# A row gradient through one DMA queue: turns of three loads and three stores become turns of two and two

## The chip, the cores and the metric

The kernel runs on one core of a Trainium2 chip. The metric is device time in microseconds of one execution, the median of several runs. A core has several engines that run on their own and wait for one another by semaphores. Four matter here: VectorE (DVE), which does the arithmetic; GpSimd (POOL), which does some tiny pieces; SyncE (SP), which only issues transfers; and the 16 DMA engines, which move data between the device memory and the core's on-chip memory.

## The reference

The input is an array `x` of 8192 x 8192 float32 values. The output is its gradient along each row:

```python
def reference(x: np.ndarray) -> np.ndarray:
    return np.gradient(x, axis=1)
```

Inside a row, output `j` is `(x[j+1] - x[j-1]) / 2`. At the two ends of a row it is the plain difference of the two outermost values. Each value is read once and written once: 268.44 MB in and 268.44 MB out.

## The kernel before

The 8192 rows are cut into `nsets` = 32 groups of 256 rows. A group is a tile of 128 partitions with two whole rows in each (16384 values, 64 KB per partition), so one load or one store of a group moves 8.39 MB. In what follows, L7 and S7 are the load and the store of group 7, and a turn is a place where the queue passes from loads to stores or back. (Names such as L70 with a higher number are lines of the code, as the profile writes them.)

There are `NB` = 3 slots in on-chip memory, and group `i` uses slot `i % 3`. A slot is 64 values longer than a group (`SH`): the load puts the group at an offset of 64, and the result is written at offset 0 of the same slot, so the shift lets the result run behind the reading in place.

For each group the work is:

- POOL subtracts at the row ends and keeps the four differences per partition in `ends` (line 70). It waits for the load.
- DVE computes half the difference of the shifted rows for the whole group in one instruction (line 76). It waits for POOL's subtraction.
- The `ends` values are copied over the two end places of each row (line 87), by POOL for groups whose number leaves 1 or 3 after division by 5, and by DVE for the others.
- SP issues the store (line 89), after that copy.

All loads (line 60) and stores are issued by SP, in program order, and go through one queue. The DMA engines work this queue off in order, each engine for its own part of every transfer. When SP waits for something, everything behind that instruction on SP waits too. The dependences are written out by hand: `chain` names for each instruction the earlier ones it needs. A load of group `i` from 3 on needs the store of group `i - 3`, which had the same slot.

Lines 64, 65 and 91 to 93 set the order of the queue. The first three loads go out at the start; after the store of every third group the next three loads are issued. The queue thus holds L0 L1 L2 S0 S1 S2 L3 L4 L5 S3 S4 S5 and so on; at the end, 32 groups not being a multiple of three, come L30 L31 S30 S31.

Of the kernel before, what the change touches and what calls it, by code (L numbers as in the profile page):

```python
# [1 line left out]

# [4 lines left out]


@with_exitstack
def kernel(  # L10
    ctx: ExitStack,
    tc: tile.TileContext,
    x: bass.AP,
    out: bass.AP,
):

    nc = tc.nc
    P = nc.NUM_PARTITIONS
    n, m = x.shape
    R = 2
    NB = 3  # L30
    SH = 64  # L31
    W = R * m
    nsets = n // (P * R)
    f32 = x.dtype

    x_sets = x.rearrange("(s p t) m -> s p (t m)", p=P, t=R)
    out_sets = out.rearrange("(s p t) m -> s p (t m)", p=P, t=R)

    pool = ctx.enter_context(tc.tile_pool(name="pool", bufs=1))
    slots = [pool.tile([P, SH + W], f32, name=f"slot{k}", tag=f"slot{k}") for k in range(NB)]  # L40
    ends = pool.tile([P, nsets, R, 2], f32, name="ends", tag="ends")
    loads, stores = [], [None] * nsets
    in_front = {}

    def chain(i, ins, *needed):

        group, engine = f"slot{i % NB}", ins.ins.engine
        keep = [o.ins for o in needed]  # L50
        if in_front.get(engine, (None,))[0] == group:
            keep.append(in_front[engine][1])
        tc.declare_no_dep(ins.ins, group=group, keep=keep, reason="implied by the needed step")
        tc.add_to_no_dep_group(group, ins.ins)
        in_front[engine] = group, ins.ins
        return ins

    def load(i):
        b = slots[i % NB]
        ins = nc.sync.dma_start(out=b[:, SH : SH + W], in_=x_sets[i])  # L60
        loads.append(chain(i, ins, *([stores[i - NB]] if i >= NB else [])))

    with tc.manual_schedule():
        for i in range(NB):
            load(i)
        for i in range(nsets):
            b = slots[i % NB]
            xin = b[:, SH : SH + W].rearrange("p (t m) -> p t m", m=m)

            ins = nc.gpsimd.tensor_sub(  # L70
                out=ends[:, i, :, :],
                in0=xin[:, :, 1 : m : m - 2],
                in1=xin[:, :, 0 : m - 1 : m - 2],
            )
            at = [chain(i, ins, loads[i])]
            ins = nc.vector._custom_dve(  # L76
                dve_ops.TENSOR_TENSOR_REDUCE_SUB_MAX,
                out=b[:, 1 : W - 1],
                in0=b[:, SH + 2 : SH + W],
                in1=b[:, SH : SH + W - 2],  # L80
                s0=0.0,
                s1=0.5,
            )
            halved = chain(i, ins, *at)
            res = b[:, 0:W].rearrange("p (t m) -> p t m", m=m)
            placer = nc.gpsimd if i % 5 in (1, 3) and i < nsets - 2 else nc.vector
            ins = placer.tensor_copy(out=res[:, :, 0 : m : m - 1], in_=ends[:, i, :, :])  # L87
            placed = chain(i, ins, halved)
            ins = nc.sync.dma_start(out=out_sets[i], in_=b[:, 0:W])
            stores[i] = chain(i, ins, placed)  # L90
            if i % NB == NB - 1:
                for k in range(i + 1, min(i + 1 + NB, nsets)):
                    load(k)


# [1 line left out]
_INS = ['x']  # L97
_OUTS = [((8192, 8192), 'float32')]


# [23 lines left out]
```

## Time and profile before

| what | value |
| --- | --- |
| median of 3 runs | 1247.86 us (1247.71 to 1247.9) |
| profiled execution: its span, the only time that is recorded for it | 1245.7 us |
| DMA queue's packets, share of 16 engines' span | 99.8% |
| mean transfer rate | 431 GB/s |
| DVE busy | 554.6 us, 45% |
| one DVE instruction of line 76 | 17.22 us, 32 of them |
| POOL busy | 8.8 us, 1% |
| SP's queue waiting for a load's slot to be stored | 373.1 us in 29 waits |
| SP's queue waiting for a result, copied by DVE / by POOL | 525.6 us in 20 waits / 300.1 us in 12 |

A view in order of time has the start in microseconds from the beginning of the span, the duration, the engine, the line, the operation and the tiles; in brackets stands how long the engine was idle before and what ended it. "SPq" is SP issuing a transfer. "x3" or "x2" is a row in which two or three like instructions are merged, with the time from the first to the end of the last. A view by windows has, for each stretch of time, its length, the busy time of DVE and POOL with the number of instructions, the TensorE clock, the share of the DMA engines and the rate. A packet is 64 KB, one engine's eighth of its part of a transfer, and counts whole in the window where it starts, so a short window can show shares over 1 and rates far over the mean. The trace also keeps the start and duration of each single packet; where a text says "packet records", these are meant.

### The profile page before, as it was taken

Reading aid. Unit: us, or ns where it says so; the run is one execution under the profiler, and the core shown is the slowest. Engines: PE = TensorE matmul, PEld = TensorE weight load, DVE = VectorE, ACT = ScalarE, POOL = GpSimd, SP = SyncE. Lnnn points to the kernel's source line nnn. Section 1 sums busy time; section 2 is a strip of 40 time slices with the busy share of each in tenths; the row PEclk is TensorE's granted clock in tenths of the full one; section 3 lists DMA queues with packets and bytes.
Section 4 is the critical chain, followed back from the end, with each engine's and each line's share of the span. In section 5 each row is a group of like instructions: output and inputs, shape, how many; then the busy total and the mean of one; then the engine's idle time right before and its main releaser. Section 6 shows DMA issues by size and latency. Waiting matters only on the chain.

```text
span 1245.7 us, 237 instructions
## 1 busy us (share of the span) xinstructions
DVE 554.6 (45%) x52; POOL 8.8 (1%) x48
## 2 busy tenths in 40 slices
DVE  2850583069009702850582079009603840591083
POOL 0000000000000000000000000000000000000000
DMA  9999999999999999999999999999999999999999
GB/s 404 438 436 423 427 431 438 438 438 436 436 427 431 425 438 436 425 434 436 429 434 436 434 436 434 436 434 438 419 436 436 434 438 438 431 434 429 429 410 404
DMA packets 9217, 536.88 MB, mean 431 GB/s; under 512 B 1024, under 2 KB 1024, under 8 KB 1024
## 3 DMA queue, kind: packets, MB, share of 16 engines
q1 hardware_dynamic: 9216, 536.88, 99.8%
q14 instruction: 1, 0.01, 0.0%
HBM read 268.44 MB, written 268.44 MB: 431 GB/s over the span
## 4 chain that ended last, share of the span: by engine, by line
another core or an unknown queue 74%; DVE 18%; DMA 3%; issue 2%; POOL 1%; SPq 0%; POOLq 0%
DVE slot L76 18%; DMA slot<-in_x_dram 3%; POOL ends L70 0%; POOL slot L87 0%; SPq L60 0%; POOLq L119 0%; DVE slot L87 0%
## 5 line engine op out<-in xcount | busy, mean ns | idle before, releaser
L76 DVE CUSTOM_DVE_ANT_0 slot<-slot 128x16382 f32<-128x16382 f32 x32 | 551.2, 17224 | 668.7 <-POOL ends L70 668.7
L70 POOL TENSOR_TENSOR ends<-slot 128x4 f32<-128x4 f32 x32 | 6.3, 198 | 989.6 <-DMA slot<-in_x_dram 989.6
L87 POOL COPY slot<-ends 128x4 f32<-128x4 f32 x12 | 2.3, 190 | 207.9 <-DVE slot L76 207.9
L87 DVE COPY slot<-ends 128x4 f32<-128x4 f32 x20 | 3.4, 172 | 0.7
L108 POOL MEMSET const-bfloat16-1.0<- 128x1 bf16 x1 | 0.1, 101 | 0.0
L108 POOL MEMSET const-uint8-127<- 128x1 uint8 x1 | 0.1, 101 | 0.0
L108 POOL MEMSET const-float32-0.0<- 128x1 f32 x1 | 0.1, 98 | 0.2 <-issue 0.2
L108 POOL MEMSET const-float32-1.0<- 128x1 f32 x1 | 0.1, 98 | 0.0
## 6 DMA issues: line engine op xcount, KB each, us to landing
slot<-in_x_dram SPq DMA_DIRECT2D x32, 58.0
out_dram<-slot SPq DMA_DIRECT2D x32, 40.4
```

What stands on the lines that cost most here:

```text
L70: ins = nc.gpsimd.tensor_sub(out=ends[:, i, :, :], in0=xin[:, :, 1 : m : m - 2], in1=xin[:, :, 0 : m - 1 : m - 2],)
L76: ins = nc.vector._custom_dve(dve_ops.TENSOR_TENSOR_REDUCE_SUB_MAX, out=b[:, 1 : W - 1], in0=b[:, SH + 2 : SH + W], in1=b[:, SH : SH + W - 2],
L87: ins = placer.tensor_copy(out=res[:, :, 0 : m : m - 1], in_=ends[:, i, :, :])
L108: nc = _bacc.Bacc("TRN2", target_bir_lowering=False, num_devices=1)
```

## The change

The order of the queue is all that changes. `turns` is the list 2, 4, 6, ... 32. Two loads go out at the start, and after the store of every second group the next two loads are issued, so the queue holds L0 L1 S0 S1 L2 L3 S2 S3 and so on to L30 L31 S30 S31: 16 turns of two and two. There are still three slots, used in rotation, so a load of group `i` still needs the store of group `i - 3`. What the engines compute, the tiles, the size of a transfer and who copies the ends stay as they were.

```diff
@@ -31,6 +22,7 @@
     SH = 64
     W = R * m
     nsets = n // (P * R)
+    turns = list(range(2, nsets + 1, 2))
     f32 = x.dtype
 
@@ -61,7 +51,7 @@
         loads.append(chain(i, ins, *([stores[i - NB]] if i >= NB else [])))
 
     with tc.manual_schedule():
-        for i in range(NB):
+        for i in range(turns[0]):
             load(i)
         for i in range(nsets):
             b = slots[i % NB]
@@ -88,8 +78,8 @@
             placed = chain(i, ins, halved)
             ins = nc.sync.dma_start(out=out_sets[i], in_=b[:, 0:W])
             stores[i] = chain(i, ins, placed)
-            if i % NB == NB - 1:
-                for k in range(i + 1, min(i + 1 + NB, nsets)):
+            if i + 1 in turns[:-1]:
+                for k in range(i + 1, turns[turns.index(i + 1) + 1]):
                     load(k)
```

## The prediction

> **What bounds the kernel now.** I read the page first: busy shares, slices, queues. Then I read the instructions in order of time, for when each load lands and each store is issued, and last the busy time of narrow windows at two places where the queue turns from loads to stores. The page:
>
> ```profile
> span 1245.7 us, 237 instructions
> DVE 554.6 (45%) x52; POOL 8.8 (1%) x48
> DMA 9999999999999999999999999999999999999999
> q1 hardware_dynamic: 9216, 536.88, 99.8%
> L76 DVE CUSTOM_DVE_ANT_0 slot<-slot 128x16382 f32<-128x16382 f32 x32 | 551.2, 17224 | 668.7 <-POOL ends L70 668.7
> ```
>
> The one queue keeps the 16 DMA engines busy for 99.8% of the span, and VectorE works 45% of it. So the time is the time of 64 transfers of 8.39 MB, one after another, and the question is what the new order does to the gaps between them. The chain of waits gives 74% to an "unknown queue" and is no help here. In order of time, POOL's subtraction (L70) starts 0.07 us after its load has landed, so its starts are the landings:
>
> ```profile
> 489.13 0.20 POOL L70 TENSOR_TENSOR ends<-slot 128x4 f32<-128x4 f32 x1 [59.56 <-DMA slot<-in_x_dram]
> 508.46 0.20 POOL L70 TENSOR_TENSOR ends<-slot 128x4 f32<-128x4 f32 x1 [19.13 <-DMA slot<-in_x_dram]
> 528.31 0.20 POOL L70 TENSOR_TENSOR ends<-slot 128x4 f32<-128x4 f32 x1 [2.14 <-DMA slot<-in_x_dram]
> 605.63 0.20 POOL L70 TENSOR_TENSOR ends<-slot 128x4 f32<-128x4 f32 x1 [77.12 <-DMA slot<-in_x_dram]
> ```
>
> These are L12, L13, L14 and L15 (L and S are the load and store of a group). L13 follows L12 by 19.33 us. L14 follows by 19.85: 0.5 us more. L15 comes 77.32 us later, four transfers (S12, S13, S14, L15) of 19.33. Every triple looks so: only its last load, the one with a store behind it in the queue, is ever late. Over the nine triples from L5 to L29 the third interval is over 19.34 by 0.11, 0.17, 0.71, 0.51, 0.45, 0.11, 0.50, -0.01 and 0.02: 2.57 us. The very first turn (L2, 62.44 - 42.04 = 20.40) cost 1.06. In the windows around it each 64 KB packet counts where it starts, so 1498 GB/s in 0.70 us is 16 packets, one of each engine:
>
> ```profile
> 57.90:58.60 0.70, 0.70 (x1) 0.00 (x0) 1.00 5.02 1498
> 58.60:60.90 2.30, 0.90 (x1) 0.19 (x1) 1.00 0.00 0
> 60.90:61.40 0.50, 0.00 (x0) 0.00 (x0) 1.00 0.00 0
> 61.40:62.10 0.70, 0.00 (x0) 0.00 (x0) 1.00 3.47 1498
> 62.10:63.80 1.70, 1.12 (x1) 0.20 (x1) 1.00 0.00 0
> 63.80:64.50 0.70, 0.70 (x1) 0.00 (x0) 1.00 3.45 1498
> ```
>
> The last packets of L2 take 3.5 us, the next ones 2.4. So a turn from loads to stores stretches the last load packet. The packet records give the same place for the later turns; there the worst engine of each loses 0.40, 0.31, 0.78, 0.92, 0.53, 0.40, 0.71, 0.06 and 0.35 us (mean 0.50), while other engines lose less and run ahead. An undisturbed packet takes 2.418 us, and 8 of them make the 19.34.
>
> **The change part by part.** Before, the queue holds L L L S S S; the first store of a triple is issued a whole transfer ahead of its turn (17.7 us after its load, with two loads behind that one). After, it holds L L S S, and the end of the trace of before already has such a pair: L30, L31, S30, S31.
>
> ```profile
> 1186.93 0.20 POOL L70 TENSOR_TENSOR ends<-slot 128x4 f32<-128x4 f32 x1 [77.07 <-DMA slot<-in_x_dram]
> 1187.17 17.22 DVE L76 CUSTOM_DVE_ANT_0 slot<-slot 128x16382 f32<-128x16382 f32 x1 [59.84 <-POOL ends L70]
> 1204.42 0.17 DVE L87 COPY slot<-ends 128x4 f32<-128x4 f32 x1
> 1204.62 19.69 SPq L89 DMA_DIRECT2D out_dram<-slot  x2
> 1206.28 0.20 POOL L70 TENSOR_TENSOR ends<-slot 128x4 f32<-128x4 f32 x1 [19.14 <-DMA slot<-in_x_dram]
> ```
>
> ```profile
> 1204.60:1205.40 0.80, 0.00 (x0) 0.00 (x0) 1.00 0.00 0
> 1205.40:1205.60 0.20, 0.00 (x0) 0.00 (x0) 1.00 11.49 4915
> 1205.60:1205.80 0.20, 0.00 (x0) 0.00 (x0) 1.00 0.00 0
> 1205.80:1206.00 0.20, 0.00 (x0) 0.00 (x0) 1.00 0.76 328
> ```
>
> *The wait that becomes tight.* Let P be the moment the subtraction of the pair's first load starts. The store is issued at P + 17.69 (1204.62 - 1186.93). Fifteen engines start it 0.78 to 0.98 us later (4915 GB/s in 0.20 us are 15 packets): at P + 18.57, say. The sixteenth was still on L31 and starts at about 1205.85, P + 18.92. So the trailing engine never waits: the store is there some 0.35 us (0.25 to 0.45) before it is needed. A group whose ends POOL places is 0.05 later (157.63 - 139.89 = 17.74), with 0.30 left. The second store has the same margin against the end of the first, and the windows at 1224.8 show no hole there. So the gap costs nothing on the trailing engine; its cover is the second load, and it is thin. If that cover goes, each 0.1 us past it costs 1.5 us over 15 new pairs. Bounds: below, 0; above, the start of the very first load, whose packets begin 1.0 to 1.7 us after its issue at 0.74, up to 0.7 later than S30's: (0.7 - 0.3) x 15 = 6. I take 0, since S30 and S31 are this very case.
>
> The Trainium skill (DMA: Bandwidth & Descriptors, Anatomy of one DMA) speaks against the change: it gives a DMA a fixed cost of about 2.0 us, fitted on GpSimd's path. By that, landing to landing, 17.7 + 2.0 = 19.7 us stand against 19.34, and the estimate is 0.35 us lost in each of 15 pairs, 5 us in all. The trace has 0.88 us ahead of the first packet and 0.43 between the last packet and the subtraction, 1.3 in all, and the measurement decides.
>
> *What is queued behind the wait.* SP's order is now store, store, load, load, and while SP waits for the first store of a pair nothing but the pair's second load is in the queue. Before, there were two loads. The second load of a pair waits for the store three groups back, which lands while the other store and the other load are still queued: nothing. The first load of a pair waits for a store two transfers further back: nothing. No instruction is added; VectorE's 17.22 us still end 1.9 us ahead of the next subtraction.
>
> *The fast engines lose their lead.* This I think costs most. Before, up to two transfers are queued at each wait, so an engine that was not held up runs on, and by L31 the first engines are 3 us ahead of the last. After, the store comes 0.35 us before the last engine needs it, so no engine gets further ahead than that, and in each pair all wait for that pair's worst engine. So the worst engine of each turn counts, and no longer only the one that is behind for good.
>
> *Terms, against the profiled span of 1245.7:*
> - The nine turns of triples go: -2.57. The first turn stays (its store is the first either way) and so does the last.
> - Fourteen turns come. Ends: 0 each (L31 to S30 took 19.35) and 1.06 each (the first turn), 0 to 14.8. If the same engine trails for good, 2.57/9 = 0.29 each, 4.0; if the worst of 16 counts in full, 0.50 each, 6.9. With a lead of 0.35 allowed it lies between: I take the middle, 5.5.
> - Turns from stores to loads: 15 instead of 10. By the packet records the worst engine loses 0.16 us on average at each of these ten, the mean engine 0.02. Then between 15 x 0.02 = 0.3 and 15 x 0.16 = 2.4; I take 1.0.
> - The first packet of S30 on an engine that stood empty took 2.45 instead of 2.418: 0.03 x 15, at most 0.4; I take it whole.
>
> Sum: -2.6 + 5.5 + 1.0 + 0.4 = +4.3 us, a span of 1250.0. The page gives the profiled execution no time but its span; the median of the runs shown, 1247.86, is 2.2 above it. I add the difference: 1247.9 + 4.3 = 1252.2.
>
> **The rivals.** A measurement of this kernel can tell about 0.2%, 2.5 us, from no change.
>
> *Nothing to see.* The trailing engine stays the same one and pays only its own stretch: 4.0 + 0.3 - 2.6 = +1.7, so 1249.6. For it: in the last four triples before L31 the landings are nearly even. Against it: the lead of the fast engines grew from 0.6 us after L0 to 3 us, and that is what the pairs would give up.
>
> *Not slower: the stretch does not occur.* The place is the turn to stores. If a stretch needs a store already queued behind the load packet, a store that comes 0.35 us ahead meets little of it; L31 to S30 shows none. Then only -2.6 + 0.4 remains, 1245.7, and with the first turn's 1.06 gone too 1244.6. It decides once a turn costs its worst engine less than about 0.1 us ((2.57 - 1.4) / 14). Against it: one turn with most engines empty is little evidence.
>
> *A wait takes the place of the queue.* The store comes late under full traffic, up to the 6 us worked out above: 1252.2 + 6 = 1258.
>
> *Turns like the first.* If 1.06 is the price of engines that turn together (they stood 0.6 us apart then), and not of a first store, all 14 pay it: 14.8 + 1.4 - 2.6 = +13.6, 1261.5. For it: the pairs keep the engines together. Against: L5 and L8, with engines 0.8 and 1.0 us apart, cost 0.11 and 0.17.
>
> **How the numbers follow.** Chances: the forecast 0.40, nothing to see 0.25, no stretch 0.15, a late store 0.12, turns like the first 0.08. Faster by over 0.2% (under 1245.4) is two thirds of "no stretch": 0.10. Within 0.2% (to 1250.4): its other third and "nothing to see": 0.30. Slower: the other three, 0.60. The range leaves out the deepest part of "no stretch" and half of "turns like the first": 1245.0 to 1262.0. The likeliest case's own range is 1250 to 1255.
>
> **What would show it.** In the profile of the changed kernel each store of a pair's first group is issued 17.7 us after its subtraction starts, and the second subtraction starts about 1.6 us after that issue. If I am right, landings within a pair stay 19.3 to 19.4 apart or gain a few tenths, and four transfers (first landing to first landing) take 77.4 plus 0.3 to 0.7. Packets of a first store start on all engines within about half a microsecond, pair after pair. A late store would show as DMA windows with no packets on every engine at once, ahead of each first store. I would be wrong if four transfers took 77.35 throughout, or over 78.2.

## The result and the profile after

The changed kernel takes 1271.58 us (median of 5 runs, 1268.16 to 1272.68) against 1247.86 for the kernel before on the same chip: a ratio of 1.0186, 95% interval 1.0175 to 1.0197. It is 23.7 us slower; the forecast was 1252.2, slower by 4.3, with a range to 1262.0. The profiled execution has a span of 1269.7 us against 1245.7, 24.0 more. The page of the changed kernel:

```profile
span 1269.7 us, 236 instructions
DVE 554.6 (44%) x52; POOL 8.8 (1%) x48
DMA  9999999999999999999999999999999999999999
q1 hardware_dynamic: 9216, 536.88, 98.9%
```

VectorE's busy time has not moved. The queue still looks full: 98.9% instead of 99.8%. But a packet that takes longer counts as busy for longer, so this share hides most of what happened. In the changed kernel the average rate is 423 GB/s instead of 431 for the same bytes. The instructions in order of time show where (L18 to L20, S18 and S19):

```profile
734.87 0.20 POOL L60 TENSOR_TENSOR ends<-slot 128x4 f32<-128x4 f32 x1 [59.98 <-DMA slot<-in_x_dram]
752.39 0.19 POOL L77 COPY slot<-ends 128x4 f32<-128x4 f32 x1 [17.32 <-DVE slot L66]
752.61 19.65 SPq L79 DMA_DIRECT2D out_dram<-slot  x2
754.23 0.20 POOL L60 TENSOR_TENSOR ends<-slot 128x4 f32<-128x4 f32 x1 [1.64 <-DMA slot<-in_x_dram]
772.36 1.69 SPq L50 DMA_DIRECT2D slot<-in_x_dram  x2
814.76 0.20 POOL L60 TENSOR_TENSOR ends<-slot 128x4 f32<-128x4 f32 x1 [60.33 <-DMA slot<-in_x_dram]
```

S18 goes out 17.74 us after L18's subtraction started, and L19 lands 1.6 us after that: this is what the prediction took from the end of the old trace. L19 follows L18 by 19.36. But L20 follows L19 by 60.53, three transfers that should take 58.03. So by the landings the time is not lost where the queue passes to stores, but between the first store and the next pair's first load. Over the run, pair to pair takes (1210.79 - 101.64) / 14 = 79.23 us instead of 4 x 19.344 = 77.38. Two narrow windows of the changed kernel show the two turns; each packet counts where it starts. First the turn to stores, L19 to S18:

```profile
749.70:751.45 1.75, 1.75 (x1) 0.00 (x0) 1.00 1.38 599
751.45:752.60 1.15, 0.88 (x1) 0.19 (x1) 1.00 0.01 0
752.60:753.45 0.85, 0.00 (x0) 0.00 (x0) 1.00 0.00 0
753.45:753.95 0.50, 0.00 (x0) 0.00 (x0) 1.00 4.91 2097
```

The 16 last packets of L19 start over 1.6 us; then the store, issued at 752.61, starts on all 16 engines within half a microsecond. The engines that were ahead waited for it, up to 1.4 us; the last one hardly did (0.07 us by the packet records). Then the turn to loads, S17 to L18, with the last two packets of S17 and the first of L18:

```profile
707.85:708.35 0.50, 0.00 (x0) 0.00 (x0) 1.00 4.84 2097
708.35:710.25 1.90, 0.00 (x0) 0.00 (x0) 1.00 0.00 0
710.25:710.80 0.55, 0.00 (x0) 0.00 (x0) 1.00 5.73 1907
710.80:713.25 2.45, 0.00 (x0) 0.00 (x0) 1.00 0.00 0
713.25:714.05 0.80, 0.00 (x0) 0.00 (x0) 1.00 3.32 1311
```

From the last packet but one to the last it is 2.4 us, and from the last to the first load packet 3.0 or more: the last packet of the store is longer by 0.4 to 1.1 us on every engine. In the kernel before this turn cost nothing. There the last two packets of S2 and the first of L3 are 2.4 us apart throughout:

```profile
114.55:115.20 0.65, 0.00 (x0) 0.00 (x0) 1.00 3.72 1613
115.20:116.95 1.75, 0.00 (x0) 0.00 (x0) 1.00 0.00 0
116.95:117.65 0.70, 0.00 (x0) 0.00 (x0) 1.00 3.45 1498
117.65:119.35 1.70, 0.00 (x0) 0.00 (x0) 1.00 0.00 0
119.35:120.05 0.70, 0.00 (x0) 0.00 (x0) 1.00 3.48 1498
```

To see all turns at once I sum, from the landings in the trace, by how much each transfer landed later than 19.344 us after the one before it, sorted by its place. In this table and in the text, "last load" is the load ahead of a store, "first store" the store behind it, "last store" the store ahead of a load, and "first load" the load behind that; the middle transfers of a triple are near zero (-0.34 us in 21).

| kernel | last loads | first stores | last stores | first loads |
| --- | --- | --- | --- | --- |
| before (11 and 10 turns) | 3.58 | 0.13 | 0.35 | -0.19 |
| changed (16 and 15 turns) | 1.04 | 1.77 | 12.28 | 12.48 |

The differences, -2.5 + 1.6 + 11.9 + 12.7, make 23.7 of the 24.0 us. So the turns to stores have become cheaper, and the turns to loads cost it all: some 0.8 us in the last store of each pair, on all engines, and some 0.8 in the next first load, there by the worst engine.

The packet records give the same sum for the average engine, as longer packets and as time without one. In the changed kernel it loses 11.1 us in the last store packets, 10.8 standing empty ahead of the first stores, 2.9 in the first load packets and 5.0 elsewhere, 29.8 in all; in the kernel before it is 6.0, of which 3.1 are in the last load packets. The difference, 23.9, is the span's. So what the landings show at the first loads, by the slowest engine, the average engine loses mostly in waiting for the next first store.

### The profile page after: what moved, and what is told of

It reads as the page before. It is cut to its first block, busy times and chain, and to the rows that moved or that the text cites. A ratio compares the mean times of both kernels' runs of the same rounds, so it can differ in the third digit from the quotient of the medians.

```text
span 1269.7 us, 236 instructions
## 1 busy us (share of the span) xinstructions
DVE 554.6 (44%) x52; POOL 8.8 (1%) x48
## 3 DMA queue, kind: packets, MB, share of 16 engines
q1 hardware_dynamic: 9216, 536.88, 98.9%
## 4 chain that ended last, share of the span: by engine, by line
DMA 52%; DVE 30%; another core or an unknown queue 13%; issue 2%; POOL 1%; SPq 0%; POOLq 0%
DMA slot<-in_x_dram 52%; DVE slot L66 30%; POOL ends L60 0%; SPq L79 0%; POOL slot L77 0%; DVE slot L77 0%; SPq L50 0%; POOLq L109 0%
```

## The experiments

Three theories stood at first. *M:* the margin is too thin; the first store of a pair is issued only as the last load ends. *T:* it is the turns, which cost this much if they come every two transfers. *B:* a load now goes out right behind a store, 0.04 to 0.11 us later and with no wait, where before it waited for a landing.

**Two and two with a third load ahead (`lead3`).** Only the lead changes:

```diff
-        for i in range(turns[0]):
+        for i in range(NB):
             load(i)
...
-            if i + 1 in turns[:-1]:
-                for k in range(i + 1, turns[turns.index(i + 1) + 1]):
+            if i % 2 == 1:
+                for k in range(i + 2, min(i + 4, nsets)):
                     load(k)
```

> Turns of two and two as in the changed kernel, but three loads go out at the start, so at each turn to stores the first store has been ready for a whole transfer and the queue never runs short. Theory M (margin: what costs is that each pair's first store is issued only as the last load ends, so the queue runs nearly empty once per pair): the 1.97 us per pair go, 1247 to 1253 us. Theory T (turns: a turn between loads and stores costs this much when it comes every two transfers, whatever the margin): as the changed kernel, 1268 to 1273 us. Theory B (a load issued 0.04 us behind a store, with no wait between, makes the last packet of that store long): 1247 to 1255 us as well, since here every load after a store waits for a landing.

Measured: 1249.42 us, ratio to before 1.0016 (1.0006 to 1.0025). With as many turns as the changed kernel, the loss is gone but for 2 us.

**Half of the work (`half_work`).**

```diff
-                out=b[:, 1 : W - 1],
-                in0=b[:, SH + 2 : SH + W],
-                in1=b[:, SH : SH + W - 2],
+                out=b[:, 1 : m],
+                in0=b[:, SH + 2 : SH + m + 1],
+                in1=b[:, SH : SH + m - 1],
```

> The changed kernel with half of VectorE's work left out: line 66 computes only the first of the two rows of each partition, the other is left unshifted. The queue's order and bytes are the same; each store is ready some 8.6 us earlier, so the margin at the first store of a pair is 9 us instead of 0.35. Theory M: 1247 to 1253 us. Theory T: 1268 to 1273. Theory B: 1268 to 1273, less what the turn to stores itself loses (some 0.5 us a pair, 8 us in all), so about 1262, since the load still goes out right behind the store.

Measured: 1249.79 us in one run, before 1247.35. The first load of each pair still goes out some 0.4 us after the issue of the second store, as in the changed kernel, and the last store packets are not longer (0.00 us by the packet records). So B falls.

**The first load is to wait (`even_wait`).**

```diff
-        loads.append(chain(i, ins, *([stores[i - NB]] if i >= NB else [])))
+        back = [stores[i - NB]] if i >= NB else []
+        if i % 2 == 0 and i >= 2:
+            back = [stores[i - 2]]
+        loads.append(chain(i, ins, *back))
```

> The changed kernel, but the first load of each pair also waits for the first store of the pair before it (which is in another slot), so it is issued about 1.4 us later, after that store has landed and while the second one moves. Theory B: the last packet of each second store is no longer 0.7 us longer, 1250 to 1258 us. Theories M and T: no change, 1268 to 1273 us.

Measured: 1270.7 us in one run. But the wait did not come about. First the changed kernel, then `even_wait`:

```profile
119.33 19.70 SPq L79 DMA_DIRECT2D out_dram<-slot  x2
139.14 1.65 SPq L50 DMA_DIRECT2D slot<-in_x_dram  x2
```

```profile
120.06 19.74 SPq L82 DMA_DIRECT2D out_dram<-slot  x2
139.85 1.57 SPq L50 DMA_DIRECT2D slot<-in_x_dram  x2
```

The first load (L4) goes out 0.05 us after the issue of S3 ends (0.11 in the changed kernel), at 139.85, though S2, which it was to wait for, lands at 141.0. So this run is in effect the changed kernel once more and says nothing on B; B fell with `half_work`. T falls by the first two runs: turns of two cost next to nothing as such if the stores come early.

**Three and three with a late first store (`late3`).** The copy of the ends and the store of a triple's first group are put off:

```diff
+            todo = [(i, res, halved, out_sets[i], b)]
+            if i % NB == 0 and i + 2 < nsets:
+                held = todo
+                continue
+            if held:
+                todo = held + todo
+                held = None
+            for q, r, h, o, t in todo:
...
```

> The kernel before, turns of three and three, but the end values of a triple's first group are placed only after VectorE's work on the second group, so that the first store is issued 17.7 us after the second load lands, just as the third load ends. The margin is now as thin as in the changed kernel, ten times instead of fifteen. Theory M: 10 x 1.97 = 20 us more than before, 1262 to 1270 us. Theory T: no change, 1247 to 1251 us. Theory B: no change or some 0.5 us a turn to stores, 1247 to 1253 us, since the load behind the third store still waits for a landing.

Measured: 1253.49 us in one run, 6.1 more than before: M was right that a late store costs time in this order too, but the sum was only a third. The table of landings says what is there and what isn't:

| kernel | last loads | first stores | last stores | first loads |
| --- | --- | --- | --- | --- |
| lead3 (16, 15) | 6.14 | 0.36 | 0.65 | -1.09 |
| half_work (16, 15) | 5.84 | 0.63 | 0.83 | -1.42 |
| even_wait (16, 15) | 0.66 | 1.59 | 12.61 | 11.74 |
| late3 (11, 10) | 0.10 | 0.37 | 7.92 | 1.49 |

In `late3` each of the ten last stores, two transfers behind the late one, loses its 0.8 us although it was itself issued a transfer ahead. And the turns to stores, which lose 3.58 in the kernel before, lose nothing. So a late store makes its own turn free and the next turn to loads dear.

**Which of a pair's two stores is late (`early_even`, `early_odd`).** In the changed kernel the second store, too, is issued only some 0.35 us before its turn. Half the work is left out for one group of each pair (`cut` is `0 if i % 2 else m` in the first kernel, `m if i % 2 else 0` in the second):

```diff
+            cut = 0 if i % 2 else m
...
-                out=b[:, 1 : W - 1],
-                in0=b[:, SH + 2 : SH + W],
-                in1=b[:, SH : SH + W - 2],
+                out=b[:, 1 : W - 1 - cut],
+                in0=b[:, SH + 2 : SH + W - cut],
+                in1=b[:, SH : SH + W - 2 - cut],
```

> The changed kernel with half of VectorE's work left out for each pair's first group only (its second row in each partition stays unshifted): the first store of a pair is issued some 9 us ahead, the second one still only 0.3 us before the first one ends. Theory D (dry: an engine needs the next transfer some time before its last packet ends; a transfer that comes later than that, though before the end, leaves its reading side empty, and the next turn from stores to loads then lasts about 0.7 us longer on every engine): the second store is late in this sense too, so the 0.74 us at each turn to loads stay, the idle gaps before first stores go; 1258 to 1263 us. Theory F (only the first store's thin margin matters, since with it the queue passes from loads to stores): 1247 to 1252 us.

> The changed kernel with half of VectorE's work left out for each pair's second group only: the first store comes as late as in the changed kernel, the second lies queued behind it some 8 us ahead. Theory D: like the three-and-three kernel with late first stores, which lost 0.79 us at the last store and 0.15 at the next load: 15 x 0.95 on top of 1247 to 1249, so 1260 to 1265 us, and the 0.83 us at each pair's first load shrink. Theory F: all of the loss stays, 1268 to 1273 us.

Measured: 1274.07 and 1268.59 us, one run each, before 1246.5. Both are far above what D gave, and `early_even`, with less work and the first store 9 us earlier, is slower than the changed kernel. F falls with `early_even`, by 22 us; its range for `early_odd` held.

| kernel | last loads | first stores | last stores | first loads |
| --- | --- | --- | --- | --- |
| early_even (16, 15) | 16.47 | 0.57 | 12.68 | 0.52 |
| early_odd (16, 15) | 0.77 | 2.20 | 10.42 | 11.02 |

The last stores lose their 0.7 to 0.85 if either store was late, as D said. What D lacked is in the first column: once the engines have run dry, the next turn to stores costs 1.03 us if its store is early. The very first turn of the kernel before (L2, 1.06) has the same size, and every run starts with an empty queue. At the first turn of the others it is 1.13 in `lead3` and 1.01 in `half_work`, whose first store is early, and 0.01 or less in the changed kernel and `late3`, where it is late. Windows of `early_even`: the last three packets of L17 and the first of S16, then the last two of S17 and the first of L18.

```profile
668.50:669.10 0.60, 0.00 (x0) 0.00 (x0) 1.00 4.03 1748
669.10:671.00 1.90, 0.00 (x0) 0.00 (x0) 1.00 0.00 0
671.00:671.55 0.55, 0.00 (x0) 0.00 (x0) 1.00 4.40 1907
671.55:673.40 1.85, 0.00 (x0) 0.00 (x0) 1.00 0.00 0
673.40:673.95 0.55, 0.00 (x0) 0.00 (x0) 1.00 6.53 1907
673.95:676.80 2.85, 0.00 (x0) 0.00 (x0) 1.00 0.00 0
676.80:677.55 0.75, 0.00 (x0) 0.00 (x0) 1.00 3.24 1398
710.95:711.35 0.40, 0.00 (x0) 0.00 (x0) 1.00 6.05 2621
711.35:713.35 2.00, 0.00 (x0) 0.00 (x0) 1.00 0.00 0
713.35:713.80 0.45, 0.00 (x0) 0.00 (x0) 1.00 6.78 2330
713.80:716.35 2.55, 0.00 (x0) 0.00 (x0) 1.00 0.00 0
716.35:717.00 0.65, 0.00 (x0) 0.00 (x0) 1.00 4.00 1613
```

Steps of 2.4 us between packets, then 3.4 at the turn to stores and 3.0 at the turn to loads.

**How much margin is needed (`sweep_up`, `sweep_mix`).** With `cut` from a list by pairs:

```diff
+            cut = 240 * (0, 1, 2, 3, 4, 5, 6, 7, 8, 10, 12, 14, 16, 20, 24, 32)[i // 2]
```

> The changed kernel with a little of VectorE's work left out, more from pair to pair: 0, 240, 480 ... 7680 of 16382 values at the end of each partition stay unshifted, 0.25 us for each 240, so the margin grows from 0.35 us in the first pair to 8.4 in the last. Theory D: a step; below some margin every pair loses its full 2 us or nearly, above it nothing. Theory G (gaps: the loss is the idle time of the engines that finished early, 0.68 us on average, passed on to the worst engine): it falls evenly with the margin and is gone from a margin of 1.0 to 1.4 us, about the fifth pair on; then the sum is 1247 to 1253 us. With a step at one packet, 2.4 us, nine pairs lose: 1249 + 9 x 1.6 = 1263.

> The same amounts of work left out as in the rising series, in another order over the pairs (8, 0, 5, 16, 2, 12, 1, 20, 4, 10, 3, 32, 6, 24, 7, 14 times 240 values), to part the margin from the place in the run and from what the pairs before have left behind. Theory D: each pair loses by its own margin, with the same step as in the rising series. Theory G: by its own margin too, but evenly, and none above 1.4 us. If the state of the pairs before decides, neighbours of pairs without margin lose as well.

Measured: 1257.29 and 1257.64 us, one run each, before 1246.5. Neither theory has it. In the rising series the first two pairs lose 2.0 us each and the last four 0.2 to 0.6, but those between lose 0.25 to 1.5 in no order. The engines end the second load up to 3.4 us apart there, so that one store can be early for some and late for others. So I went to single engines in the mixed series: for each engine and pair the shorter of the two times from a store's issue to the end of that engine's packet before it, and how much longer than 2.418 us the last packet of the pair's second store was, by the packet records. (These name no engine; a packet is taken to follow the one that ended just before it.)

| issue to packet's end, us | engines x pairs | last store packet longer by, mean us |
| --- | --- | --- |
| under 0.5 | 23 | 0.76 |
| 0.5 to 1.0 | 21 | 0.95 |
| 1.0 to 1.2 | 18 | 0.68 |
| 1.2 to 1.6 | 27 | 0.28 |
| 1.6 to 2.0 | 26 | 0.23 |
| 2.0 to 2.4 | 27 | 0.08 |
| over 2.4 | 98 | 0.00 |

It is no step; it fades between 1.0 and 2.2 us, and is gone at about the time of one packet. Of this time 0.85 us goes by before a packet can start at all (S30 in the trace of before: 0.84 to 0.97 on the 15 engines that stood ready). The changed kernel's 0.35 us beyond that is 1.2 in this table's terms: too little for the last engine by about 1 us, and far too little for those ahead of it. G's limit, 1.0 to 1.4 us beyond the start, was about right, but not its reason: three pairs of the mixed series had no idle time on any engine at the turn to stores (pairs 4, 8 and 14, counted from 0) and their last store packets were still 0.36 to 0.55 us longer. The pairs with wide margins that follow lose up to 1.39 us in their last load packets, the price of coming back that `early_even` had shown; with it, from second load to second load, those three pairs lost 1.4 to 1.9.

**Two single faults (`late_twice`).** To have the whole course without neighbours, two triples of the kernel before get a late first store:

```diff
-            if i % NB == 0 and i + 2 < nsets:
+            if i in (9, 21):
```

> The kernel before, turns of three and three, with the first store held back until VectorE is done with the second group in two triples only (groups 9 and 21). Theory D2 (a store issued less than one packet, 2.4 us, before an engine's last load packet ends leaves that engine empty once; it then loses 0.7 us at its next turn to loads, and about 1.0 at the first turn to stores after that whose store is early again, as the very first turn did; then the turns are free again): in both places nothing at the turn to the late store, 0.7 us in the last packet of S11 and of S23, 1.0 in the last packet of L14 and of L26, and the usual 0 to 0.6 further on; about 2 x 1.7 less what these turns lose anyhow, 1249 to 1251 us. Rival D1 (a late store costs its 0.7 at the next turn to loads and nothing is to be won back): no 1.0 at L14 and L26, 1248 to 1249 us.

Measured: 1251.0 us in one run, before 1247.96. The windows at the first fault: the last two packets of S11 and the first of L12; the last two of L14 and the first of S12; the last of S14 and the first of L15.

```profile
463.80:464.20 0.40, 0.00 (x0) 0.00 (x0) 1.00 6.06 2621
464.20:466.20 2.00, 0.00 (x0) 0.00 (x0) 1.00 0.00 0
466.20:466.60 0.40, 0.00 (x0) 0.00 (x0) 1.00 7.75 2621
466.60:469.15 2.55, 0.00 (x0) 0.00 (x0) 1.00 0.00 0
469.15:469.85 0.70, 0.00 (x0) 0.00 (x0) 1.00 3.65 1498
522.45:522.95 0.50, 0.50 (x1) 0.00 (x0) 1.00 4.84 2097
522.95:524.85 1.90, 1.90 (x1) 0.00 (x0) 1.00 0.00 0
524.85:525.40 0.55, 0.55 (x1) 0.00 (x0) 1.00 6.31 1907
525.40:528.30 2.90, 0.99 (x1) 0.19 (x1) 1.00 0.00 0
528.30:529.00 0.70, 0.00 (x0) 0.00 (x0) 1.00 3.47 1498
583.80:584.50 0.70, 0.00 (x0) 0.00 (x0) 1.00 3.45 1498
584.50:586.25 1.75, 0.00 (x0) 0.00 (x0) 1.00 0.00 0
586.25:586.95 0.70, 0.00 (x0) 0.00 (x0) 1.00 3.47 1498
```

At S11 the step is 3.0 us instead of 2.4, at L14 3.4, and at S14 2.4 again. By the packet records the mean of 16 engines is 0.68 and 1.05 us at the first fault, 0.75 and 1.07 at the second, and 0.00 at the last stores after that; in the kernel before, L14 and L26 lose 0.63 and 0.01 in these packets. This is D2 in place, size and order: one late store, 0.7 us at the next turn to loads, 1.05 at the next turn to an early store, then free turns to loads and the usual 0 to 0.6 at turns to stores. D1 falls.

**Half stores (`split2`, `split3`).** Rows worked and stored one by one (VectorE copies all the ends here):

```diff
+            stores[i] = []
+            for t in range(R):
+                lo, hi = t * m, (t + 1) * m
...
+                    out=b[:, lo + 1 : hi - 1],
+                    in0=b[:, SH + lo + 2 : SH + hi],
+                    in1=b[:, SH + lo : SH + hi - 2],
...
+                ins = nc.vector.tensor_copy(out=b[:, lo : hi : m - 1], in_=ends[:, i, t, :])
...
+                ins = nc.sync.dma_start(out=out_sets[i, :, lo:hi], in_=b[:, lo:hi])
```

> The changed kernel with the whole computation, its two rows of each partition worked and stored one after the other: two VectorE instructions of half the length, each followed by its ends and a store of 4.19 MB. The first half store of a pair is issued some 8.6 us sooner, the second has that half store ahead of it. The order of loads and stores in the queue, turns of two groups and two groups, is the changed kernel's. Theory D2: the loss goes, 1247 to 1253 us. If turns of two cost time by themselves, or packets of 32 KB do: 1258 us or more.

> The kernel before with the same halves. Theory D2: the first store of a triple is early anyway, so there is nothing to win but perhaps part of the 2.6 us that its turns to stores lose: 1244 to 1249 us. If the smaller packets cost time: over 1250 us.

Measured: 1252.01 us for two and two, ratio to before 1.0036 (1.0022 to 1.0050), and 1250.80 for three and three, 1.0022 (1.0013 to 1.0032). With the whole computation and the changed kernel's order of loads and stores, the earlier stores win back 20 of the 24 us. In three and three the halves cost 2.8 us; their smaller packets may be the reason, which was not tested apart. None of the kernels beats the one before.

## Why the prediction was wrong

*The bound.* Right: the queue's transfers are the time, and VectorE's and POOL's instructions kept theirs.

*The wait that becomes tight: this is the step that failed.* Its times were right (store issued at P + 17.7, engines that stood ready starting mostly 0.84 to 0.99 us later, the last engine idle for 0.08 us at most). What failed is the sentence "So the gap costs nothing on the trailing engine", and behind it "I take 0, since S30 and S31 are this very case". The case was not the same: S30 and S31 are the last transfers, so no turn to loads follows them, and that is where a late store is paid. The rate of a packet stream that shows no hole also said nothing on what the engine needs ahead of a packet's end: by the mixed series about 2.2 us from the issue, where this order leaves 1.2.

*Terms.* Four transfers took 79.23 us, over the 78.2 that the prediction named as a sign of being wrong. The turns from stores to loads were put at 1.0 us and measured 12.28 + 12.48 in the landings. They were priced by ten rows of a queue that never ran short, between 0.3 and 2.4, and the bounds were those of the wrong state. The turns to stores were put at 5.5 - 2.6 = +2.9; they measured 1.04 + 1.77 - 3.58 - 0.13 = -0.9. The rival "the stretch does not occur" thus held for these turns, as L31 to S30 had hinted, and its gain of 2.5 us drowned. For the rival "nothing to see" the prediction called the landings of the last four triples nearly even; by its own list L23 was 0.50 us late there.

*The fast engines lose their lead.* The mechanism held: the 16 engines start each first store within 0.24 to 0.85 us, and stand empty for 0.68 us on average before it, 10.8 us in all, so each pair does go by its worst engine. What it multiplies was misplaced: the worst engine falls behind in the first load packet (by 0.4 to 1.7 us), not in the last one, and the prediction had that turn at 1.0 us in all. `half_work` and `lead3`, in which the engines keep their leads, lose 5.8 to 6.1 us at the turns to stores and nothing at the others.

*The rival "a wait takes the place of the queue"* had the right place, the late store, and the wrong signs. It looked for windows without packets on every engine; there were none, as the price is paid in longer packets a transfer or more later. Its 6 us were bounded by late starts alone. The estimate from the Trainium skill (DMA: Bandwidth & Descriptors, Anatomy of one DMA), 2.0 us fixed for each DMA and 5 us in all, pointed the right way: an order with 0.35 us to spare has nothing to spare. The runs here put the measured need at 2.2 to 2.4 us from issue to the end of the packet before, and the price at some 1.6 us a pair. That 2.0 and 2.2 are near is no confirmation: the first is a transfer's own start and completion, for which the trace has 1.3, the second a lead over the packet before.

*"Turns like the first"* took the first turn's 1.06 us for a price of engines that turn together. In `lead3` the engines are 0.6 us apart at L2 and still at L4; L2, the first turn, lands 1.13 us late and L4 0.01. So it is not that. The single faults show the same price again where the queue comes back from running short.

*Open.* Half of the loss, the 12.48 us at first loads, follows from the late first store of a pair: it is there in `early_odd` (11.02) and gone in `early_even` (0.52). It goes with the time that the average engine stands empty before first stores: 9.9 us in `early_odd`, 0.04 in `early_even`, 1.3 in `late3`. By the packet records the stretch falls unevenly, on 3 to 11 of the 16 engines by over 0.1 us, up to 1.7 us in a first load packet. Why triples with a late first store have so little of it (1.49 in ten turns) is not settled. Why the engines behave as they do inside is not shown either; the runs show when a packet becomes longer, not what it waits for.

## What to carry to other kernels

In a transfer-bound kernel like this one, measure how long before the end of the running transfer the next one is issued, and keep that over a packet's time (here 2.4 us, of which the start alone takes 0.85); that a queue has no visible holes is not enough. Ask what the queue holds at the moment of each wait: three slots in turns of two leave one load there, in turns of three two, and with a third load ahead the turns of two are nearly as good (1249.4 us). And before a short piece of the trace is taken for a whole new order, look at whether what follows it in the new order follows it there too.

## What the runs showed that was not expected

A queue that runs short leaves a state behind. In this state a turn to loads costs each engine some 0.7 us; a first turn to an early store costs 1.05 us and ends it, after which turns to loads are free (0.00 in the last store packet) and turns to stores cost 0 to 0.6. A late store at a turn costs little there (0.37 us in the landings of `late3`, 1.77 in those of the changed kernel, over all turns), but the state stays. So making one of two late stores early can cost time: `early_even`, which pays both prices in each pair, was the slowest kernel of all at 1274.07 us.
